# A hybrid encoder layer on one core: when the second half of the cross-attention keys is loaded and split, and where the normalisation of the memory is applied

## The chip, the cores and the metric

The kernel runs on one core of a Trainium2 chip. The metric is the device time of one execution in microseconds (us). In this text PE is TensorE, DVE is VectorE, ACT is ScalarE, POOL is GpSimd and SP is SyncE, the engine whose queue issues most of the loads. Each engine works through its own queue strictly in order; what waits at the head of a queue holds all that stands behind it.

## The reference

One layer with three residual sub-layers, on 1024 rows of width 1024 and a memory of 256 tokens, all in float32:

```python
mem_n = rms_norm(mem, mem_g)
y_ssm = s5_mixer(u, ...)                      # state space branch, 512 channels
y_fox = forgetting_attention(q, k, v, f_logit) # 8 heads of 64, causal
y_mix = concat([rms_norm(y_ssm), rms_norm(y_fox)])
x = x + rms_norm(y_mix @ w_out, mix_post_g)

h = rms_norm(x, xa_pre_g)                     # 4 heads of 256, 256 memory tokens
kv = mem_n @ wkv                              # keys: first 1024 columns, values: the rest
p = softmax((h @ wq) @ k.T / sqrt(256))
x = x + rms_norm((p @ v) @ wo, xa_post_g)

h = rms_norm(x, ffn_pre_g)
x = x + rms_norm((silu(h @ w_gate) * (h @ w_up)) @ w_down, ffn_post_g)
```

`rms_norm(mem)` multiplies each memory token by one number, the reciprocal root of its mean square, and each column by a gain. The number of a token is a constant of a whole column of `kv` transposed, so it can be applied to the memory before the product `mem_n @ wkv` or to the product behind it.

## The kernel before, in words

Every float32 product is made of three products of halves: a tile is *split* (`split`, L112 to L119) into a high part, rounded by ACT (L113), and a low part, the difference, made by DVE (L115, or L117 where a gain is multiplied in), and `mm3` (L121 to L124) adds high x high, high x low and low x high in one PSUM bank. So each tile that PE reads costs ACT and DVE one instruction each, and PE waits for the later of the two.

The program runs in stages: the input projection with the state space scan, the eight heads of the forgetting attention (their scores run from 231.8 to 468 us), the output projection (its additions run from 494.6 to 551.6 us), the cross attention, and the feed-forward part, which takes the rest. The attention heads are paced with *fillers*, other work that is stepped between them: among these `mem_load` (L955), which reads the memory, the sixteen `mem_tile`s (L971), each of which makes one 128-row tile of `kv` transposed and stores it in DRAM (`kv_d`), and `build_a(0)`.

`mem_load` first spreads the 256 reciprocal roots over all partitions (`row_bcast`, L169, two transposes on PE and an ACT copy, into a tile `rb` of the tag `t2`). Then for each of the eight slices of the memory DVE multiplies by `rb` in place (L965), and the slice is split with its gain (L113, L117). In `mem_tile` a weight tile is loaded and split (`load_w`, L155; its load is L159 and its tile `raw`, the split tile `whl`), 24 matmuls fill a bank, ACT copies it to a tile `t` (L977), and POOL issues the store.

The cross attention needs its query weights folded with the keys, `build_a(c)` for the two halves c of the heads (L1001), and its output weights folded with the values, `value_weights(h)` for the four heads (L1041). `build_a` loads the keys of a head from `kv_d` (L1008), splits them, loads and splits two tiles of query weights, and makes eight f32 tiles in four banks, each split with a gain into a `slab`. `build_a(0)` is one of the fillers. `value_weights(0)` and `(1)` are stepped between the halves of the output projection's tiles (L1054 to L1091); `value_weights(2)`, `build_a(1)` and `value_weights(3)` come at its end.

The loop over the output projection (L1060) goes through the tiles 3, 4, 5, 6, 7, 0, 1, 2. Each tile loads the state space part into `t` (tags `a` and `b` in turn, L1070) and the rows of `x` into `xt` (tags `e` or `c`, L1073), does two times twelve matmuls, adds (L1080), squares (ACT, L1082), multiplies by a gain (POOL, L1084), takes the reciprocal root (`rsqrt_mean`, ACT L137 and L138, DVE L139 to L145) and forms the residual (DVE, L1088). Tiles 3 to 7 are stored (POOL, L1092), tiles 0 to 2 stay in SBUF. Tile 7, the last one in the tag `e`, is stored from there.

The order of each engine's queue isn't written by hand: a scheduler sets it when the program is built, by its own estimates of time and by priorities, and the queues are then fixed. `tc.issue_after(i)` tells it that an instruction has to stand behind `i` in the order in which they are issued; it makes no wait at run time. Tiles come from pools with a fixed number of buffers for each tag: 2 of `a`, 2 of `b`, 3 of `c`, 1 of `d`, 1 of `e`, 3 of `t2`, 2 of `yt`, 2 of `raw`, 3 of `whl`, and 4 banks of `g`. An instruction that writes a tile waits for the last reader of the buffer's previous tile.

Of the kernel before, what the change touches and what calls it, by code (L numbers as in the profile page):

```python
# [10 lines left out]
F32R = mybir.dt.float32r  # L11
# [6 lines left out]
P = 128  # L18
S = 1024
D = 1024  # L20
# [32 lines left out]
def layer(ctx: ExitStack, tc: tile.TileContext, a, out):  # L53
# [113 lines left out]
        return v[:, 0], v[:, 1]  # L167

    def row_bcast(r, n):  # L169
        rb = t2t([P, n * P]) if n == 2 else tt("d", [P, n * P])  # L170
        ps = (s_ps if n > 4 else g_ps)([P, n * P])
        for j in range(n):
            pe.transpose(ps[:, j * P:(j + 1) * P], r[:, j:j + 1].broadcast_to([P, P]), ident)
        for j in range(0, n, 4):
            cs = slice(j * P, min(j + 4, n) * P)
            act.activation(out=rb[:, cs], in_=ps[:, cs], func=AF.Copy)
        return rb
# [778 lines left out]
    def mem_load(r, out):  # L956
        rb = row_bcast(r, 2)
        yield
        mh, ml = slab([P, KT, 256]), slab([P, KT, 256])
        for k in range(0, KT, 4):  # L960
            m = raw([P, 4, 256])
            sp.dma_start(out=m, in_=a["memT"].rearrange("(k p) m -> p k m", p=P)[:, k:k + 4])
            for kk in range(4):
                with behind():
                    dve.tensor_tensor(out=m[:, kk], in0=m[:, kk], in1=rb, op=ALU.mult)  # L965
                    split(mh[:, k + kk], ml[:, k + kk], m[:, kk], g_mem[:, k + kk:k + kk + 1])
                if kk % 2:
                    yield
        out.extend((mh, ml))

    def mem_tile(i, mh, ml):  # L971
        wh, wl = load_w(a["wkv"][i], P, stage="e" if i % 3 == 2 else None)
        ps = g_ps([P, 256])
        for k in range(KT):
            mm3(ps, wh[:, k], wl[:, k], mh[:, k], ml[:, k], k == 0, k == KT - 1)
        o = t2t([P, 256])
        act.activation(out=o, in_=ps, func=AF.Copy)  # L977
        stB.dma_start(out=kv_d[i], in_=o)


# [16 lines left out]
        yield from build_a(0)  # L997

    Ah, Al = {}, {}

    def build_a(c):  # L1001
        for t in range(2):
            Ah[c, t], Al[c, t] = slab([P, 4, 512]), slab([P, 4, 512])
        for h in range(2):
            hd = 2 * c + h
            kh = tt(("ea", "ba")[c][h], [P, 2, 2, 256], F32R)
            kr = kh[:, 1].bitcast(F32)
            sp.dma_start(out=kr, in_=kv_d[2 * hd:2 * hd + 2].rearrange("d p m -> p d m"))  # L1008
            split(kh[:, 0], kh[:, 1], kr)
            wq = [load_w(a["wqT"][2 * hd + d], P) for d in range(2)]  # L1010
            ms = slice(h * 256, h * 256 + 256)
            for ft in range(0, KT, 2):
                ps = g_ps([P, 2, 256])
                for f in range(2):
                    for d in range(2):
                        mm3(ps[:, f], wq[d][0][:, ft + f], wq[d][1][:, ft + f], kh[:, 0, d], kh[:, 1, d], d == 0, d == 1)
                for f in range(2):
                    split(Ah[c, ft // 4][:, ft % 4 + f, ms], Al[c, ft // 4][:, ft % 4 + f, ms], ps[:, f],
                          g_xa[:, ft + f:ft + f + 1])
                yield  # L1020
# [44 lines left out]
    for n, j in enumerate((3, 4, 5, 6, 7, 0, 1, 2)):  # L1065
        ts = slice(j * P, (j + 1) * P)
        t = tt("ab"[n % 2])
        with tc.issue_after(wo_read.ins) if n else ExitStack():
            for i in range(2):
                sp.dma_start(out=t[64 * i:64 * i + 64], in_=t1_d.rearrange("j (k s) d -> s k j d", s=16)[2 * j + i])  # L1070
        xt = tt("ec"[n % 4 > 0])
        with tc.issue_after(wo_read.ins):
            sp.dma_start(out=xt, in_=a["x"][ts, :])  # L1073
        ss4, ss, r = sm(4, "ss4"), sm(1, "ss"), sm(1, "r")
        for h in range(2):
            hs = slice(h * 512, h * 512 + 512)
            ps = x_ps([P, 512])
            for k in range(4):
                mm3(ps, yf[k][:, 0, ts], yf[k][:, 1, ts], wo[k][:, 0, hs], wo[k][:, 1, hs], k == 0, k == 3)
            dve.scalar_tensor_tensor(out=t[:, hs], in0=ps, scalar=r_f[:, j:j + 1], in1=t[:, hs], op0=ALU.mult, op1=ALU.add)  # L1080
            for q in range(2 * h, 2 * h + 2):
                act.activation(out=tt("yt", [P, 256]), in_=t[:, q * 256:q * 256 + 256], func=AF.Square,  # L1082
                               accum_out=ss4[:, q:q + 1])
            pool.tensor_tensor(out=t[:, hs], in0=t[:, hs], in1=g_mp[:, hs], op=ALU.mult)  # L1084
            step(between)
        dve.tensor_reduce(out=ss, in_=ss4, op=ALU.add, axis=mybir.AxisListType.X)
        rsqrt_mean(r, ss, D)
        dve.scalar_tensor_tensor(out=xt, in0=t, scalar=r, in1=xt, op0=ALU.mult, op1=ALU.add)  # L1088
        if j < 3:
            kept[j] = xt  # L1090
        else:  # L1091
            stC.dma_start(out=x1_d[j], in_=xt)  # L1092
# [546 lines left out]
```

## Time and profile before

| | |
|---|---|
| median of three runs | 1417.84 us (1416.02 to 1421.99) |
| the profiled execution, whole | 1418.36 us |
| its span in the profile | 1416.6 us |
| mean granted clock of PE | 0.989 of full speed |
| PE busy in the span | 97% |
| DVE, ACT, POOL busy | 67%, 46%, 27% |

PE is busy for nearly the whole span, and the stages differ in what the other engines have to do, so a share of the whole says little about one place. The rows of a timeline give the start, the duration, the engine, the line, the operation and the tiles (written<-read); a bracket at a row's end tells how long the engine had been idle before it and what released it. Rows with SPq are the moments at which SP's queue issues a transfer. Durations of matmuls are those of one from its first row to its last result and overlap; the distance of two starts is what one costs.

### The profile page before, as it was taken

To read this page: it belongs to the slowest core of one execution; us is meant where nothing else is said; L and a number is where in the kernel's file an instruction comes from. 1 tells how busy PE (TensorE), PEld (TensorE's weight loads), DVE (VectorE), ACT (ScalarE), POOL (GpSimd) and SP (SyncE) were. 2 spreads that over 40 slices of the span, in tenths; PEclk is the share of its full clock that TensorE was granted. 3 is DMA by queue.
4 is the path that set the end of the run, shared out by engine and by line. 5 is a ranking of instruction groups with operands and counts; after the bars stand their busy time and mean duration, and the time that the engine had idled before them with its cause. 6 is when DMAs were issued, how large, how long until landed. Compare 5 with 4: busy or idle time off the path is not lost.

```text
span 1416.6 us, 19877 instructions
## 1 busy us (share of the span) xinstructions
PE 1378.3 (97%) x7161; PEld 1150.5 (81%) x7161; DVE 949.1 (67%) x1719; ACT 650.1 (46%) x1273; POOL 377.3 (27%) x430
## 2 busy tenths in 40 slices
PE   9999989999999996999999999999999999999997
PEld 7889888779978785888888788888888888888886
DVE  8949944947667676535457677777766676565566
ACT  7383345856556545534334533333333334444441
POOL 0011110001111152002021367676666661000021
PEclk9999999989999998999999999999999999999999
DMA  6435665348672764024457255554444446965544
GB/s 216 150 109 154 208 221 136 96 130 237 192 198 87 220 207 138 31 74 149 164 175 270 97 186 186 182 189 147 151 156 156 169 151 223 336 225 196 179 164 164
DMA packets 104627, 241.52 MB, mean 170 GB/s; under 512 B 11528, under 2 KB 40200, under 8 KB 104336
## 3 DMA queue, kind: packets, MB, share of 16 engines
q1 hardware_dynamic: 86000, 178.33, 40.1%
q0 software_dynamic: 18528, 61.91, 12.1%
q8 instruction: 56, 0.92, 0.3%
q14 instruction: 43, 0.35, 0.1%
HBM read 171.52 MB, written 79.43 MB: 177 GB/s over the span
## 4 chain that ended last, share of the span: by engine, by line
PE 59%; ACT 0%; DVE 0%; DMA 0%; issue 0%; DVEq 0%; ACTq 0%
PE x L1304 17%; PE g L1304 13%; PE x L1567 7%; PE g L1567 7%; PE g L124 2%; PE g L122 2%; PE g L123 2%; PE x L122 2%; PE x L124 2%; PE x L123 2%; PE g L1100 1%; PE g L1211 1%; DMA raw<-in_wqT 0%; ACT whl L113 0%; DVE whl L115 0%
## 5 line engine op out<-in xcount | busy, mean ns | idle before, releaser
L1304 PE MATMUL x<-slab,op 128*128 128x512 f32 x984 | 233.2, 389 | 0.5 <-DVE op L115 0.5
L1304 PEld LDWEIGHTS x<-slab,op 128*128 128x128 f32 x984 | 184.6, 188 | 39.3 <-DVE op L115 1.0
L1304 PE MATMUL g<-slab,op 128*128 128x512 f32 x744 | 178.7, 389 | 0.0
L115 DVE TENSOR_TENSOR slab<-slab 128x1024 fp32r<-128x1024 f32 (+2 forms) x96 | 115.1, 1208 | 83.1 <-ACT slab L113 81.6
L1304 PEld LDWEIGHTS g<-slab,op 128*128 128x128 f32 x744 | 139.6, 188 | 29.0
L122 PE MATMUL g<-slab,whl 128*128 128x512 f32 (+1 forms) x416 | 151.6, 364 | 0.8 <-ACT slab L487 0.4
L123 PE MATMUL g<-slab,whl 128*128 128x512 f32 (+1 forms) x416 | 148.4, 357 | 0.0
L124 PE MATMUL g<-slab,whl 128*128 128x512 f32 (+1 forms) x416 | 148.3, 357 | 0.0
L113 ACT ACTIVATE slab<-slab 128x1024 fp32r<-128x1024 f32 (+2 forms) x96 | 99.3, 1039 | 103.7 <-DMA slab<-hs_d 78.1
L1567 PE MATMUL g<-slab 128*128 128x512 f32 x462 | 126.7, 389 | 0.0
L1567 PE MATMUL x<-slab 128*128 128x512 f32 x462 | 126.7, 389 | 0.0
L1567 PEld LDWEIGHTS x<-slab 128*128 128x128 f32 x462 | 86.7, 188 | 18.0
L1567 PEld LDWEIGHTS g<-slab 128*128 128x128 f32 x462 | 86.7, 188 | 18.0
L115 DVE TENSOR_TENSOR op<-slab,op 128x512 fp32r<-128x512 f32 x80 | 85.6, 1080 | 11.2 <-ACT op L113 10.9
L1380 POOL TENSOR_TENSOR wt<-wt 128x256 f32<-128x256 f32 x88 | 81.5, 927 | 26.2 <-DMA wt<-in_w_down 22.8
L122 PEld LDWEIGHTS g<-slab,whl 128*128 128x128 f32 x416 | 78.7, 189 | 12.0 <-ACT whl L113 0.6
L124 PEld LDWEIGHTS g<-slab,whl 128*128 128x128 f32 x416 | 78.4, 189 | 11.6 <-DVE whl L115 0.2
L123 PEld LDWEIGHTS g<-slab,whl 128*128 128x128 f32 x416 | 78.7, 189 | 10.6
L113 ACT ACTIVATE op<-slab 128x512 fp32r<-128x512 f32 x80 | 50.2, 629 | 80.6 <-PE x L1304 38.6
L113 ACT ACTIVATE op<-ss 128x512 fp32r<-128x512 f32 x60 | 37.7, 631 | 91.9 <-PE g L1304 55.7
L115 DVE TENSOR_TENSOR whl<-raw,whl 128x1024 fp32r<-128x1024 f32 (+2 forms) x58 | 64.5, 1118 | 20.9 <-ACT whl L113 20.6
L1407 POOL TENSOR_TENSOR ss<-slab 128x512 f32<-128x512 f32 x40 | 62.2, 1554 | 58.3 <-DMA slab<-in_w_up 25.9
(395 smaller groups left out, 2891.7 us busy)
## 6 DMA issues: line engine op xcount, KB each, us to landing
hs_d<-ev POOLq DMA_DIRECT2D x77, 256.0 KB, 2.6
slab<-hs_d SPq DMA_DIRECT2D x35, 512.0 KB, 4.0
wt<-in_w_down SPq DMA_DIRECT2D x44, 256.0 KB, 3.5
wt_d<-wt POOLq DMA_DIRECT2D x22, 512.0 KB, 4.8
slab<-in_w_gate SPq DMA_DIRECT2D x20, 512.0 KB
slab<-in_w_up SPq DMA_DIRECT2D x20, 512.0 KB, 5.1
slab<-wt_d SPq DMA_DIRECT2D x20, 512.0 KB, 8.2
wd_d<-in_w_down SPq DMA_DIRECT2D x33, 256.0 KB, 4.8
```

The lines of the kernel that those rows point to most:

```text
L113: first = act.activation(out=hi, in_=src, func=AF.Copy, scale=1.0 if mul is None else mul)
L115: (lo_eng or dve).tensor_tensor(out=lo, in0=src, in1=hi.bitcast(F32), op=ALU.subtract)
L122: pe.matmul(ps, lh, rh, start=first, stop=False)
L123: pe.matmul(ps, lh, rl, start=False, stop=False)
L124: pe.matmul(ps, ll, rh, start=False, stop=last)
L1100: pe.transpose(tp[:, k], src[:, (k0 + k) * P:(k0 + k + 1) * P], ident)
L1211: turned = pe.transpose(tp[:, k], h3[:, (4 * n + k) * P:(4 * n + k + 1) * P], ident)
L1304: pe.matmul(ps, x[:, k], y[:, k], start=first and k + n == 0, stop=k == 3 and n == 2, skip_group_check=not first)
L1380: pool.tensor_tensor(out=o, in0=x, in1=y, op=ALU.subtract)
L1407: made[0] = pool.tensor_tensor(out=o, in0=x, in1=y, op=fn)
L1567: pe.matmul(banks[n][j], xo[:, u, js], wo[:, v], start=ends[0] and k == 0, stop=ends[1] and k == 2, skip_group_check=onto is not None)
```

## The change

Three edits. First, the second half of the keys (`build_a(1)`) uses the tile tags `e` and `b` instead of `b` and `a`, and its two loads are issued behind the last load of `x` in the output projection (`x_read[0]`), its two splits behind the last reciprocal root there (`x_read[1]`, the ACT instruction of L137 or L138 that comes first). Second, DVE's eight products L965 go; the row constant `rb` is kept until the last `mem_tile`, and the eviction of each of the sixteen banks, an ACT copy before, is a DVE product with `rb` (L976 in the new numbering). Third, `rb` moves from the tag `t2` to the tag `yt`. Behind the places of the diff the line numbers move by one to two.

```diff
     def row_bcast(r, n):
-        rb = t2t([P, n * P]) if n == 2 else tt("d", [P, n * P])
+        rb = tt("yt", [P, n * P]) if n == 2 else tt("d", [P, n * P])
...
             for kk in range(4):
                 with behind():
-                    dve.tensor_tensor(out=m[:, kk], in0=m[:, kk], in1=rb, op=ALU.mult)
                     split(mh[:, k + kk], ml[:, k + kk], m[:, kk], g_mem[:, k + kk:k + kk + 1])
...
-        out.extend((mh, ml))
+        out.extend((mh, ml, rb))

-    def mem_tile(i, mh, ml):
+    def mem_tile(i, mh, ml, rb):
...
         o = t2t([P, 256])
-        act.activation(out=o, in_=ps, func=AF.Copy)
+        dve.tensor_tensor(out=o, in0=ps, in1=rb, op=ALU.mult)
         stB.dma_start(out=kv_d[i], in_=o)
...
+    x_read = [None, None]
...
-            kh = tt(("ea", "ba")[c][h], [P, 2, 2, 256], F32R)
+            kh = tt(("ea", "eb")[c][h], [P, 2, 2, 256], F32R)
             kr = kh[:, 1].bitcast(F32)
-            sp.dma_start(out=kr, in_=kv_d[2 * hd:2 * hd + 2].rearrange("d p m -> p d m"))
-            split(kh[:, 0], kh[:, 1], kr)
+            with tc.issue_after(x_read[0].ins) if c else ExitStack():
+                sp.dma_start(out=kr, in_=kv_d[2 * hd:2 * hd + 2].rearrange("d p m -> p d m"))
+            with tc.issue_after(x_read[1].ins) if c else ExitStack():
+                split(kh[:, 0], kh[:, 1], kr)
...
-            sp.dma_start(out=xt, in_=a["x"][ts, :])
+            x_read[0] = sp.dma_start(out=xt, in_=a["x"][ts, :])
...
-        rsqrt_mean(r, ss, D)
+        x_read[1] = rsqrt_mean(r, ss, D)[0]
```

What the scheduler makes of it shows in the queues. The first place is ACT's queue at the end of the output projection, before the change. The splits of keys write `a` and `b` (128x512); the split that writes `t_5682` belongs to the values of the third head (`value_weights(2)`); `yt,ss<-a` and `yt,ss<-b` are the squares of the last two tiles, `slab<-g` an eviction of `value_weights`.

```order
L113 ACTIVATE a<-a 128x512
L137 ACTIVATE rsy<-ss,epsc 128x1
L138 ACTIVATE rsy<-rsy 128x1
L1082 ACTIVATE yt,ss_5550<-a 128x256 x2
L113 ACTIVATE whl<-raw 128x1024
L1082 ACTIVATE yt,ss_5550<-a 128x256 x2
L113 ACTIVATE b<-b 128x512
L137 ACTIVATE rsy<-ss,epsc 128x1
L138 ACTIVATE rsy<-rsy 128x1
L113 ACTIVATE slab<-g 128x512
L1082 ACTIVATE yt,ss_5618<-b 128x256 x2
L113 ACTIVATE t_5682<-t_5683 128x512
```

The same place after the change. The values' split is now `t_5674`, the keys' tiles are `e` and `b`.

```order
L138 ACTIVATE rsy<-rsy 128x1
L113 ACTIVATE slab<-g 128x512
L1084 ACTIVATE yt,ss_5610<-b 128x256 x2
L113 ACTIVATE t_5674<-t_5675 128x512
L113 ACTIVATE whl<-raw 128x1024
L113 ACTIVATE slab<-g 128x512
L1084 ACTIVATE yt,ss_5610<-b 128x256 x2
L113 ACTIVATE slab<-g 128x512
L137 ACTIVATE rsy<-ss,epsc 128x1
L113 ACTIVATE slab<-g 128x512
L138 ACTIVATE rsy<-rsy 128x1
L113 ACTIVATE e<-e 128x512
```

The first split of keys stood eleven rows ahead of the values' split, the second five; now both stand behind it, eight and nine rows (the second, `b<-b`, follows the last row shown).

The second place is SP's queue there, before the change. `c<-in_x` are the last two loads of `x`, `a<-kv_d` and `b<-kv_d` the keys, `raw<-in_wqT` a tile of query weights, `t_5835` the values of the fourth head.

```order
L1073 DMA c<-in_x 128x1024
L1008 DMA a<-kv_d 128x2x256
L1073 DMA c<-in_x 128x1024
L1008 DMA b<-kv_d 128x2x256
L159 DMA raw<-in_wqT 128x1024
L1044 DMA t_5835<-kv_d 128x2x256
L159 DMA raw<-in_wo 128x1024
```

After the change:

```order
L1075 DMA c<-in_x 128x1024 x2
L1009 DMA e<-kv_d 128x2x256
L1009 DMA b<-kv_d 128x2x256
L159 DMA raw<-in_wqT 128x1024
L1046 DMA t_5827<-kv_d 128x2x256
L159 DMA raw<-in_wo 128x1024
```

One load of keys moved behind the last load of `x`, and the tiles are others; behind the keys the queue is the same.

The third place is DVE's queue where the memory is loaded, before the change. L965 is the product with the row constant, `slab<-raw,gains` the low half of a slice, `sv_s<-g` the copy of a sum of squares out of a bank, L743 the scaling of a softmax tile.

```order
L965 TENSOR_TENSOR raw<-raw,t_2765 128x256 x4
L742 RECIPROCAL nlr<-nlr 128x1
L117 SCALAR_TENSOR_TENSOR slab<-raw,gains,slab 128x256 x3
...
L117 SCALAR_TENSOR_TENSOR slab<-g,gains,slab 128x256
L742 RECIPROCAL nlr<-nlr 128x1
L117 SCALAR_TENSOR_TENSOR slab<-raw,gains,slab 128x256 x2
L743 TENSOR_SCALAR c<-c,nlr 128x896
L240 COPY sv_s<-g 128x8
```

After the change:

```order
L742 RECIPROCAL nlr<-nlr 128x1
L117 SCALAR_TENSOR_TENSOR slab<-raw,gains,slab 128x256 x2
...
L117 SCALAR_TENSOR_TENSOR slab<-g,gains,slab 128x256
L742 RECIPROCAL nlr<-nlr 128x1
L743 TENSOR_SCALAR c<-c,nlr 128x896
L117 SCALAR_TENSOR_TENSOR slab<-raw,gains,slab 128x256 x2
L115 TENSOR_TENSOR whl<-raw,whl 128x1024
L240 COPY sv_s<-g 128x8
```

The products are gone, and the low half of a weight tile (`whl`, L115) has come to stand directly ahead of the copy `sv_s`. In the memory tiles themselves each ACT row L977 is gone and a DVE row L976 stands in its place. From the middle of the cross attention on the queues are the same as before.

## The prediction

> **What bounds the kernel now.** I read the page first, then who TensorE (PE) waits for in the first 600 us, then stretches, then each queue's timeline around the longest wait.
>
> ```profile
> PE 1378.3 (97%) x7161; PEld 1150.5 (81%) x7161; DVE 949.1 (67%) x1719; ACT 650.1 (46%) x1273; POOL 377.3 (27%) x430
> ```
>
> PE is busy for 1378.3 of 1416.6 us. So only two things can be won: some 38 us in which it stands, and stretches in which its clock is halved. The waits of PE up to 600 us:
>
> ```profile
> PE g L122 <- ACT t L113: 10.8, 1, 10.8
> PE g L760 <- DVE sv_s L240: 1.8, 1, 1.8
> PE g L239 <- ACT slab L765: 1.8, 1, 1.8
> PE g L122 <- ACT slab L765: 1.4, 1, 1.4
> ```
>
> One wait of 10.8 us stands out (place B, the end of the output projection). The three others lie within 10 us of each other (place A, where the memory is loaded). The same in stretches; the last three columns are the granted clock, the DMA share and GB/s:
>
> ```profile
> 539.00:556.00 17.00, 6.18 (x17) 4.55 (x16) 12.34 (x21) 9.62 (x29) 7.81 (x4) 0.60 0.32 97
> 278.00:293.00 15.00, 10.10 (x44) 7.69 (x46) 10.23 (x25) 10.00 (x20) 1.08 (x2) 0.66 0.57 167
> 331.00:403.00 72.00, 72.00 (x583) 65.51 (x583) 45.88 (x91) 40.33 (x81) 11.64 (x19) 1.00 0.72 211
> 541.00:542.00 1.00, 0.00 (x0) 0.00 (x0) 0.94 (x2) 0.42 (x3) 0.00 (x0) 0.91 0.00 0
> 555.00:556.00 1.00, 1.00 (x4) 0.80 (x4) 0.00 (x0) 0.57 (x2) 0.00 (x0) 0.77 0.72 213
> ```
>
> At both places the clock falls as well (0.60, 0.66). In the memory tiles (331 to 403, place M) PE never stands. Now B, PE first:
>
> ```profile
> 538.90 0.39 PE L123 MATMUL g<-whl,t 128*128 128x512 f32 x1
> 539.13 0.39 PE L124 MATMUL g<-whl,t 128*128 128x512 f32 x1
> 550.34 0.80 PE L122 MATMUL g<-whl,t 128*128 128x512 f32 x1 [10.82 <-ACT t L113]
> 550.93 0.63 PE L123 MATMUL g<-whl,t 128*128 128x512 f32 x1
> 551.36 0.63 PE L122 MATMUL g<-whl,t 128*128 128x512 f32 x1
> 558.30 0.28 PE L122 MATMUL g<-b,whl 128*128 128x256 f32 x1
> 561.09 0.39 PE L124 MATMUL g<-b,whl 128*128 128x256 f32 x1 [0.84 <-DVE whl L115]
> 565.16 1.03 PE L1100 MATMUL g<-ident,c 128*128 128x128 f32 x8
> 572.30 0.39 PE L122 MATMUL g<-a,whl 128*128 128x256 f32 x1
> ```
>
> PE stops at 539.52 and resumes at 550.34, with 0.43 us from one matmul to the next where it had 0.23. The 0.91 of 541 to 542 means that the clock halves at about 541.8 (0.18 us at half makes 0.91). The 0.77 of 555 to 556 puts its return at about 555.5. What PE waits for is ScalarE's (ACT) split of the third head's values, and ACT had been held:
>
> ```profile
> 540.40 0.63 ACT L113 ACTIVATE a<-a 128x512 fp32r<-128x512 f32 x1 [10.02 <-DMA a<-kv_d]
> 549.67 0.61 ACT L113 ACTIVATE t<-t 128x512 fp32r<-128x512 f32 x1
> ```
>
> ACT stood 10.02 us (from 530.38) for a load of keys that PE first reads at 572.30 (`a,whl`), with the projection's evictions queued behind it. The loads come from SP:
>
> ```profile
> 528.14 0.38 SPq L1008 DMA_DIRECT2D a<-kv_d  x1
> 533.84 0.33 SPq L1073 DMA_DIRECT2D c<-in_x  x1
> 544.14 0.38 SPq L1008 DMA_DIRECT2D b<-kv_d  x1
> 546.35 0.33 SPq L159 DMA_DIRECT2D raw<-in_wqT  x1
> SPq L1008 <- DVE c L1088: 9.9, 1, 9.9
> ```
>
> The load took from 528.14 to 540.40, 12.3 us, behind others. SP then stood 9.9 us before the other half of the keys, whose buffer waited for the evictions that ACT held up.
>
> **The change part by part: B.** In the new order ACT's split `t<-t` has neither key split ahead of it. What else stands ahead of it is squares, two root pairs, a weight split and an eviction, some 6 us of ACT work between 530.4, where ACT fell idle (540.40 - 10.02), and 539.5, and PE's own matmuls feed it at the old pace. It must still wait for its buffer, whose last reader is the matmul of 539.13. So it starts at about 539.5, takes 0.61, and PE resumes at 540.2: 10.1 us are won. The remaining gap of 0.7 us is far below the 2.3 us after which the clock fell (539.52 to 541.8), so the half clock from 550.34 to 555.5 goes too: 5.1 us at half speed are 2.5 us. Gain so far 12.6.
>
> What is late next: the keys. Their two loads now stand behind both last loads of x, and the first needs tile `e`, which POOL is still storing:
>
> ```profile
> 529.21 0.60 POOL L1092 DMA_DIRECT2D x_d<-e  x1
> x_d<-e POOLq DMA_DIRECT2D x1, 512.0 KB, 7.7
> 542.83 1.28 DVE L1088 SCALAR_TENSOR_TENSOR c<-b,r,c 128x1024 f32<-128x1024 f32 x1
> 557.82 1.06 ACT L113 ACTIVATE whl<-raw 128x1024 fp32r<-128x1024 f32 x1
> 559.82 1.22 DVE L115 TENSOR_TENSOR whl<-raw,whl 128x1024 fp32r<-128x1024 f32 x1
> ```
>
> The store lands at 529.21 + 7.7 = 536.9, so SP issues both key loads by 537.5 and the next weights (`in_wqT`) by 538. Everything that was in flight had landed by 541, so I put the keys' landing at 542 to 543 and the weights' at 545. PE reaches the keys at 540.2 + 24 x 0.23 = 545.7. ACT has the key splits done by then (two of 0.63 behind the first evictions); the weight split ends at about 547.1 and VectorE's (DVE) low half at about 549.5, since the key subtractions (2 x 0.7) and a 1.3 us residual stand ahead of it. PE can do 6 of its 48 matmuls of 0.12 us (half of 0.23 for half the columns) with the first weight tile alone, to 546.4, and 9 more without the second's low half. That makes stalls of 0.7 (to 547.1) and 1.3 (548.2 to 549.5), or 2.0 where 0.84 stood: a loss of 1.2. Bounds: nothing, and the 6 us of the first rival below. The moved loads cost SP nothing else: behind them in its queue stand only those weights, the next head's values and its weights.
>
> **A.** Eight DVE products go:
>
> ```profile
> L965 DVE TENSOR_TENSOR raw<-raw,t x8: 410/419/422, 273.6 to 277.0; 128x256 f32<-128x256 f32 x8
> 281.38 0.33 SPq L159 DMA_DIRECT2D raw<-in_wkv  x1
> 283.64 0.16 DVE L240 COPY sv_s<-g 128x8 f32<-128x8 f32 x1
> 284.84 1.06 ACT L113 ACTIVATE whl<-raw 128x1024 fp32r<-128x1024 f32 x1 [0.71 <-DMA raw<-in_wkv]
> 286.53 0.80 PE L122 MATMUL g<-whl,slab 128*128 128x512 f32 x1 [1.35 <-ACT slab L765]
> 282.00:283.00 1.00, 0.06 (x1) 0.00 (x0) 1.00 (x4) 0.38 (x1) 0.00 (x0) 0.70 0.78 119
> ```
>
> That is 8 x 0.419 = 3.4 us out of a DVE queue that is full (1.00 of 282 to 283) and ends in the copy `sv_s`, which frees a PSUM bank for PE. But the order now puts a weight split (1.2 us, with its load and ACT's half before it) ahead of that copy. Its buffer comes free about 5 us earlier without the products; load 3.5 us (281.38 to 284.84), ACT 1.06, DVE 1.2 lead to a copy at about 282.9, 0.75 earlier. ACT's weight split then no longer stands between the copy and the eviction for which PE waits at 286.53: another 1.06. Gain 1.8. The clock had halved in 282 to 283 (0.70), some 4.5 us after PE's last long matmul; the thin stretch still lasts over 6 us, so I take nothing for the clock. Bounds: 0, and the whole jam (second rival).
>
> **M.** Sixteen ACT copies become DVE products, their row constant now held until the last tile:
>
> ```profile
> L977 ACT ACTIVATE t<-g x16: 360/364/369, 331.1 to 402.6; 128x256 f32<-128x256 f32 x16
> L115 DVE TENSOR_TENSOR slab<-g,slab 128x512 fp32r<-128x512 f32 x2 | 1.4, 688 | 0.7 <-ACT slab L113 0.7
> L115 DVE TENSOR_TENSOR t<-t,t 128x512 fp32r<-128x512 f32 x1 | 0.7, 685 | 0.0
> ```
>
> A product from PSUM costs DVE what one from SBUF does (688 against 685 ns), so I price it as the old one: 16 x 0.42 = 6.7 us. DVE goes from 45.88 to some 52.6 of 72 us beside a PE that is always busy; ACT loses 5.8. The softmax units run two ahead, which hides it. If that cover is gone, all 6.7 lie on the path; less than nothing isn't possible, as PE has no idle time there. Nearest row: PE 72.00 of 72.00. I take a loss of 0.5.
> [...]
>
> Sum: 12.6 - 1.2 + 1.8 - 0.5 = 12.7. The profiled execution took 1418.36 and would take 1405.7. The median of the three runs shown, 1417.84, is 0.5 lower, so I forecast 1405.2. (0.5%, 7.1 us, is about what a measurement of this kernel can tell from no change.)
>
> **The rivals.**
> *The wait moves to the keys.* If the first key load takes the 12.3 us of the old one, it lands at 549.2, PE waits from 545.7 to 549.8 and 1.9 more for the weights behind it, and the clock halves again (2.5). Of 12.6 then 4.1 stay; with A and M 5.4: 1412.5. For it: that transfer's row. Against: it was slow in a full queue, and the new one meets an empty one (DMA share 0.00 in 541 to 542). It decides from a landing after about 544.5. 0.13.
> [...]
> *The jam at A goes altogether*: waits 1.8 + 1.8 + 1.4 and about 3 us of half clock (286.53 to 292.7), 8 in place of 1.8: 1399. For it: DVE's queue was the limit. Against: the split now ahead of the copy. 0.12.
> *Not what it says*: issue order is no wait, and ACT may meet another late load before `t<-t`, so the long wait stays: 1416.5. Against: nothing ahead of it there waits for a load directly but one weight split, whose load was issued long before. 0.05.
> *Slower*: at M each product waits in DVE's in-order queue for the tile's last matmul, with the softmax of the next units behind it, and PE then waits for those. To end 0.5% slower it must cost (12.7 + 0.5 + 7.1) / 16 = 1.3 us of PE per tile; at 1.5 the time is 1428. For it: DVE was already 1.00 busy in parts. Against: 20 us of spare DVE time there, and ACT stood for none of the copies it replaces. 0.04.
>
> **How the numbers follow.** Forecast 0.66, with 1402 to 1409 as its own range (A 0 to 3, keys 0 to 3, M 0 to 2). The range of 8 in 10 goes on to the jam's case and the keys' case: 1399 to 1412.5. Faster: 0.66 + 0.12 = 0.78. Same: both cases near 1412 to 1416, 0.17. Slower 0.05.
>
> **What would show it.** Right: in the new trace ACT's `t<-t` starts within 1 us of the matmul that frees its buffer, the gap at B is about 0.7 with clock 1.00, the key splits run after the first evictions of the third head, and a PE wait of about 2 us stands before or in the keys' matmuls. At A the copy `sv_s` comes about 1 us sooner. Wrong: a wait of several us on `e<-kv_d` or `in_wqT` at the keys, a gap over 2.3 us at B, or PE waiting in the memory tiles for DVE.

## The result, and the profile after

The changed kernel takes 1405.64 us (median of 5 runs, 1402.18 to 1407.31), the kernel before beside it 1416.02 us (5 runs, 1414.55 to 1421.99): a ratio of 0.9915, with a 95% interval of 0.989 to 0.9941. The forecast was 1405.2. The span of the profiled execution went from 1416.6 to 1403.9 us, 12.7 less, which is the sum that was forecast; but the terms of that sum were not all right, and some of the 12.7 is chance: the two medians, taken side by side, differ by 10.4. (A correction to the section on the change: `x_read[1]` is the second ACT instruction of the reciprocal root, L138.)

PE's busy time on the page is what it was, so what went is idle time in the balance (B's matmuls take 1.5 us less, since the clock stays up there, and those of the heads up to the 14th mask take 1.6 us more, 38.09 for 36.50, with the clock at 0.96 there for 1.00); the second view is the waits of PE in the changed kernel (time in all, times, longest).

```profile
PE 1378.3 (98%) x7161; PEld 1150.4 (82%) x7161; DVE 956.5 (68%) x1727; ACT 645.0 (46%) x1257; POOL 379.1 (27%) x430
```

```profile
PE g L124 <- DVE t L115: 1.6, 2, 1.1
PE g L760 <- ACT d L784: 1.0, 1, 1.0
PE g L122 <- DVE slab L115: 0.6, 1, 0.6
PE g L122 <- ACT t L113: 0.6, 1, 0.6
PE g L122 <- ACT slab L765: 0.6, 1, 0.6
```

The wait for ACT's `t`, 10.8 us before, is 0.6. The waits of 1.8 for `sv_s` and 1.8 for L239 are gone, the 1.4 for `slab` L765 is 0.6, and a 1.0 for `d` L784 has come. To see what each place gave, both traces need marks that don't move. The heads' mask matmuls (L735) are 64 in both; these are the first, the 14th, the 21st and the last, before and then after, and the first transpose behind the keys (before: the row of 565.16 in the prediction).

```profile
231.98 0.23 PE L735 MATMUL s<-maskb,identb 128*128 128x128 bf16 x1
269.95 0.23 PE L735 MATMUL s<-maskb,identb 128*128 128x128 bf16 x1
306.83 0.23 PE L735 MATMUL s<-maskb,identb 128*128 128x128 bf16 x1
461.83 0.23 PE L735 MATMUL s<-maskb,identb 128*128 128x128 bf16 x1
```

```profile
230.92 0.23 PE L735 MATMUL s<-maskb,identb 128*128 128x128 bf16 x1
270.47 0.23 PE L735 MATMUL s<-maskb,identb 128*128 128x128 bf16 x1
304.15 0.23 PE L735 MATMUL s<-maskb,identb 128*128 128x128 bf16 x1
459.56 0.23 PE L735 MATMUL s<-maskb,identb 128*128 128x128 bf16 x1
552.52 0.71 PE L1102 MATMUL g<-ident,c 128*128 128x128 f32 x5
```

The distances between them, for all kernels of this study (us; the last column is the span less the last mark):

| kernel | to 1st mask | 1st to 14th | A: 14th to 21st | heads' rest: 21st to 64th | B: 64th to transposes | rest |
|---|---|---|---|---|---|---|
| before | 231.98 | 37.97 | 36.88 | 155.00 | 103.33 | 851.4 |
| after | 230.92 | 39.55 | 33.68 | 155.41 | 92.96 | 851.4 |
| keys_only | 229.00 | 37.97 | 36.62 | 156.07 | 92.72 | 851.1 |
| mem_only | 231.96 | 37.95 | 34.17 | 155.62 | 103.25 | 851.0 |
| tags_only | 229.29 | 37.97 | 34.05 | 156.83 | 101.76 | 851.2 |
| splits_only | 228.62 | 37.98 | 33.36 | 158.30 | 92.91 | 851.3 |
| clock_fill | 228.82 | 39.57 | 36.67 | 155.97 | 104.08 | 851.3 |
| clock_fill2 | 231.61 | 37.96 | 37.52 | 154.68 | 102.36 | 851.4 |
| mem_heavy | 231.93 | 37.97 | 34.08 | 155.28 | 96.00 | 851.1 |
| pool_scale | 229.51 | 39.54 | 37.45 | 155.90 | 102.16 | 851.1 |
| copy_first | 228.71 | 39.53 | 33.65 | 155.56 | 92.34 | 851.1 |
| query_behind | 229.48 | 38.01 | 33.05 | 155.30 | 103.65 | 851.6 |
| query_later | 229.10 | 37.97 | 33.79 | 154.03 | 93.32 | 851.2 |
| all_orders | 228.41 | 38.00 | 32.75 | 154.04 | 93.29 | 851.2 |

The first two columns hold no edit of the change, and they vary by 3.6 and 1.6 us on their own. So of the 12.7 us, B gave 10.4 and A 3.2, the heads' rest took 0.4, and chance took 0.5 (1.1 won before the heads, 1.6 lost at their start). The other columns vary without an edit, too: B is 102.16 to 103.33 in before, mem_only and pool_scale, which are alike there, and the heads' rest 154.68 to 155.97 in before, clock_fill and clock_fill2, which are alike in it. So the 0.4 can't be told from chance, and B's gain is known to about 1 us.

B in the changed kernel, in order of time: SP's load of the first keys, ACT's split of the third head's values and of the first keys, and all stops of PE in the stretch (the first of them belongs to the second head's values; before the change it is 0.59 us).

```profile
536.35 0.38 SPq L1009 DMA_DIRECT2D e<-kv_d  x1
```

```profile
537.76 0.62 ACT L113 ACTIVATE t<-t 128x512 fp32r<-128x512 f32 x1
543.34 0.62 ACT L113 ACTIVATE e<-e 128x512 fp32r<-128x512 f32 x1
```

```profile
516.86 0.74 PE L124 MATMUL g<-whl,t 128*128 128x512 f32 x2 [1.10 <-DVE t L115]
538.43 0.50 PE L122 MATMUL g<-whl,t 128*128 128x512 f32 x1 [0.62 <-ACT t L113]
540.61 0.72 PE L124 MATMUL g<-whl,t 128*128 128x512 f32 x2 [0.51 <-DVE t L115]
545.97 0.39 PE L122 MATMUL g<-e,whl 128*128 128x256 f32 x1 [0.26 <-ACT whl L113]
547.33 0.39 PE L122 MATMUL g<-e,whl 128*128 128x256 f32 x1 [0.62 <-DVE slab L115]
548.47 0.39 PE L124 MATMUL g<-e,whl 128*128 128x256 f32 x1 [0.28 <-DVE whl L115]
```

The split starts at 537.76, within 0.1 us of the moment at which PE stops (538.43 - 0.62 = 537.81), without a wait for a load, and PE stops for 0.62 us. The keys' stops are 0.26 + 0.62 + 0.28 = 1.16 where 0.84 stood. The stretch from the end of the heads to the transposes as a whole, before and after (PE busy first; third from last the granted clock):

```profile
482.33:565.16 82.83, 70.58 (x346) 58.03 (x346) 52.51 (x95) 36.77 (x118) 30.90 (x23) 0.92 0.63 184
```

```profile
480.07:552.52 72.45, 69.06 (x346) 56.27 (x345) 52.97 (x95) 36.21 (x118) 29.15 (x23) 1.00 0.70 211
```

The same 346 matmuls stand idle for 12.25 us before and 3.39 after, and are busy 1.52 us less, since the clock stays up. A as a whole, before and after:

```profile
269.95:306.83 36.88, 31.96 (x183) 24.11 (x181) 23.28 (x64) 23.95 (x54) 2.17 (x4) 0.86 0.47 143
```

```profile
270.47:304.15 33.68, 31.94 (x182) 24.02 (x181) 20.99 (x56) 23.60 (x54) 2.17 (x4) 0.90 0.52 157
```

PE is busy for the same time, so all of A's gain is time in which it stood. The stops after the change, PE and then DVE:

```profile
282.55 1.61 PE L760 MATMUL g<-ident,c 128*128 128x128 f32 x5 [1.00 <-ACT d L784]
284.74 0.79 PE L122 MATMUL g<-whl,slab 128*128 128x512 f32 x1 [0.58 <-ACT slab L765]
```

```profile
282.33 1.22 DVE L115 TENSOR_TENSOR whl<-raw,whl 128x1024 fp32r<-128x1024 f32 x1
283.47 0.16 DVE L240 COPY sv_s<-g 128x8 f32<-128x8 f32 x1
```

The weight tile's low half stands right ahead of the copy, as the order showed. In the memory tiles:

```profile
331.00:403.00 72.00, 70.83 (x568) 64.03 (x568) 51.77 (x108) 37.27 (x67) 11.75 (x19) 1.00 0.70 207
```

```profile
L976 DVE TENSOR_TENSOR t<-g,yt 128x256 f32<-128x256 f32 x16 | 6.8, 423 | 7.5 <-PE g L124 7.2
```

DVE is busy for 51.77 of 72 us (45.88 before, 52.6 forecast). PE stands 1.17 us here, all of it in one stop for the softmax at 402.45, behind the tiles; before, that stop is 0.95 us at 404.70, outside of the window.

### The profile page after: what moved, and what is told of

It is laid out like the page before. It is cut to its first block, busy times and chain, and to the rows that moved or that the text cites. A ratio compares the mean times of both kernels' runs of the same rounds, so it can differ in the third digit from the quotient of the medians.

```text
span 1403.9 us, 19877 instructions
## 1 busy us (share of the span) xinstructions
PE 1378.3 (98%) x7161; PEld 1150.4 (82%) x7161; DVE 956.5 (68%) x1727; ACT 645.0 (46%) x1257; POOL 379.1 (27%) x430
## 3 DMA queue, kind: packets, MB, share of 16 engines
q0 software_dynamic: 18528, 61.91, 12.3%
## 4 chain that ended last, share of the span: by engine, by line
PE 60%; DVE 1%; ACT 0%; DMA 0%; issue 0%; DVEq 0%; ACTq 0%
PE x L1306 17%; PE g L1306 13%; PE x L1569 7%; PE g L1569 7%; PE g L124 2%; PE g L122 2%; PE g L123 2%; PE x L122 2%; PE x L123 2%; PE x L124 2%; PE g L1102 1%; PE g L1213 1%; DMA raw<-in_wqT 0%; DVE whl L115 0%; ACT whl L113 0%
## 5 line engine op out<-in xcount | busy, mean ns | idle before, releaser
L115 DVE TENSOR_TENSOR slab<-slab 128x1024 fp32r<-128x1024 f32 (+2 forms) x96 | 115.3, 1208 | 82.3 <-ACT slab L113 80.1
L115 DVE TENSOR_TENSOR op<-slab,op 128x512 fp32r<-128x512 f32 x80 | 88.5, 1117 | 10.4 <-ACT op L113 10.1
L123 PEld LDWEIGHTS g<-slab,whl 128*128 128x128 f32 x416 | 79.0, 190 | 10.7
L115 DVE TENSOR_TENSOR whl<-raw,whl 128x1024 fp32r<-128x1024 f32 (+2 forms) x58 | 66.0, 1144 | 18.4 <-ACT whl L113 18.1
```

What stands on the lines that cost most here:

```text
L115: (lo_eng or dve).tensor_tensor(out=lo, in0=src, in1=hi.bitcast(F32), op=ALU.subtract)
L123: pe.matmul(ps, lh, rl, start=False, stop=False)
```

## The experiments

The theory: ACT works in order, a split that waits for a load holds all behind it (10.02 us in the kernel before), and B's gain comes from the place of the key splits alone. The rivals: the tiles and SP's order do it; the keys become late; DVE is held in the memory tiles.

**keys_only**: the changed kernel with the three memory edits undone (products L965 back, eviction by ACT, `rb` in `t2`).

> The edits of the keys alone; the memory is scaled as before the change. Theory (ACT's in-order queue: a split that waits for a load holds the values' split behind it): the whole gain at the end of the output projection, 10.4 us by the trace of the changed kernel, and none at the memory: a ratio to the kernel before of about 0.9925, PE's gap before the third head's values under 1 us, the waits of 1.8, 1.8 and 1.4 at the memory load back. Rival (the gain needs both parts, because the memory tiles now end earlier): under 8 us, and a wait of more than 2 us at the keys.

Measured: 1406.9 us, ratio 0.9941 (0.9919 to 0.9962). B takes 92.72, 10.6 less than before; A 36.62, as before. PE's gap before the third head's values is 1.56 us, not under 1, and the waits at the memory load are 1.8, 1.0 and 2.1. For B's gain the theory holds, and the parts don't need each other.

**mem_only**: the changed kernel with the key edits undone (tags `ba`, no `issue_after`).

> The edits of the memory alone; the keys are loaded and split as before the change. Theory: at the memory load 3.2 us are won and in the memory tiles 0.4 lost, 2.8 us in all or a ratio of 0.998, and the wait for the third head's values is back at 10 to 11 us. Rival: that wait shortens by more than 2 us too, because all loads come earlier.

Measured: 1414.81, ratio 0.9984 (0.9972 to 0.9996). A gains 2.7, the heads' rest loses 0.6, B is 103.25 with its wait of 10.9. As the theory has it.

**tags_only**: which edit of the keys it is.

```diff
-            with tc.issue_after(x_read[0].ins) if c else ExitStack():
-                sp.dma_start(out=kr, ...)
-            with tc.issue_after(x_read[1].ins) if c else ExitStack():
-                split(kh[:, 0], kh[:, 1], kr)
+            sp.dma_start(out=kr, ...)
+            split(kh[:, 0], kh[:, 1], kr)
```

> The changed kernel without the two orders behind x: the keys have the new tiles, their loads stand in SP's queue where the change puts them, but both splits stand ahead of the values' split in ACT's queue. Theory: ACT stands again, from about 529 until the loads of 536.4 have landed (about 541), PE's gap is 8 to 11 us, and the time is within 3 us of the kernel before less the 2.8 of the memory part: 1413 to 1418. Rival (what counts is that SP and the tile buffers are no longer held): a gap under 3 us and about 1407.

Measured: 1411.23, ratio 0.996 (0.9946 to 0.9975), a little under the theory's range of times, and a gap a little under its 8 us. The load by SP, the split by ACT and PE's stop:

```profile
536.33 0.38 SPq L1008 DMA_DIRECT2D e<-kv_d  x1
```

```profile
539.25 0.63 ACT L113 ACTIVATE e<-e 128x512 fp32r<-128x512 f32 x1 [5.71 <-DMA e<-kv_d]
```

```profile
545.10 0.80 PE L122 MATMUL g<-whl,t 128*128 128x512 f32 x1 [7.17 <-ACT t L113]
```

SP's order is that of the changed kernel, and PE still stops for 7.17 us: B gains only 1.6. The load landed 2.9 us after its issue, not 12.3: the first rival of the prediction falls with that.

**splits_only**: the reverse; of the key edits only the place of the splits is kept.

```diff
-            kh = tt(("ea", "eb")[c][h], [P, 2, 2, 256], F32R)
+            kh = tt(("ea", "ba")[c][h], [P, 2, 2, 256], F32R)
...
-            with tc.issue_after(x_read[0].ins) if c else ExitStack():
-                sp.dma_start(out=kr, ...)
+            sp.dma_start(out=kr, ...)
```

> The changed kernel with the old tiles for the keys (b and a) and their loads not ordered behind x: of the key edits only the splits' place in ACT's queue is left. Theory: the splits' place is all, so the time is that of the changed kernel, 1404 to 1407, with stalls of at most 2 us at the keys. Rival (tiles and loads matter too): SP stands for the buffer of b again, the weights behind it come late, and PE waits 3 us or more at the keys: 1409 or more.

Measured: 1403.84, ratio 0.9912 (0.9891 to 0.9933), just under the theory's 1404. The second load of keys and the values' split:

```profile
532.55 0.39 SPq L1008 DMA_DIRECT2D b<-kv_d  x1
```

```profile
536.42 0.62 ACT L113 ACTIVATE t<-t 128x512 fp32r<-128x512 f32 x1
```

B takes 92.91. SP no longer stands long for the buffer of `b`, because ACT no longer holds the evictions that free it: this load is issued 0.42 us after the load of `x` ahead of it (532.13), where SP stood 9.9 us before the change. New tiles and the loads' order bring nothing: the place of the two splits is the whole of B. (The edit moves the DVE half of each split with the ACT half; that ACT's half is what counts is read from the rows, where ACT waits for the load and PE for ACT.)

**clock_fill** and **clock_fill2**: the price of the half clock. The kernel before, with matmuls that fill PE's gap.

```diff
         for c in range(2):
             tiles = [...]
+            if h == 2 and c == 0:
+                for _ in range(40):                      # 52 in clock_fill2
+                    pe.matmul(tiles[0][1], yf[0][:, 0, 0:P], wo[0][:, 0, 0:512], start=True, stop=True)
             for d in range(2):
```

> The kernel before, with 40 more matmuls that PE does while it waits for the third head's values (their bank is overwritten by the product that follows; nothing is left out). The wait for ACT stays as long, but PE doesn't idle through it. Theory (the half clock behind the gap costs 2.5 us): the granted clock stays at 1.00 from 541 to 556, the values' product takes about 5.5 us in place of 8.0 up to the keys, the keys wait no more than 1 us longer, and the ratio is 0.998 to 0.999. Rival (the keys behind it wait for the other engines anyway): the stall before the keys' low half grows from 0.8 to over 2.5 us, and nothing is won.

Measured: 1417.33, ratio 0.9991 (0.9978 to 1.0004). It did not test what it should: PE still stopped twice, and the clock fell at about 550.

```profile
549.32 0.50 PE L122 MATMUL g<-whl,t 128*128 128x512 f32 x1 [2.16 <-ACT t L113]
551.71 0.80 PE L124 MATMUL g<-whl,t 128*128 128x512 f32 x1 [1.66 <-DVE t L115]
```

```profile
550.00:552.00 2.00, 0.34 (x2) 0.29 (x2) 2.00 (x3) 1.61 (x6) 1.39 (x2) 0.52 0.00 0
```

> As clock_fill, with 52 such matmuls in place of 40: 11.8 us of them from 537.9 to about 549.7, so that PE has no idle stretch over 2 us at the end of the output projection (40 left 2.2 and 1.7 us close together, and the clock fell all the same). Theory (the half clock there cost 1.5 to 2.5 us in the kernel before): the granted clock stays at 1.00 to the keys, and the stretch from the end of the heads to the transposes of the cross attention takes 81 to 82 us where it took 82.8 before. Rival (what is behind it waits for the other engines anyway): 82.5 us or more at full clock.

Measured: 1418.08, ratio 0.9997 (0.998 to 1.0013). Now the clock stays at 1.00:

```profile
541.00:556.00 15.00, 13.87 (x61) 11.18 (x60) 12.95 (x24) 9.77 (x31) 7.93 (x4) 1.00 0.31 84
```

The stretch from the end of the heads takes 81.85 (82.83 before): B gains 1.0, the upper part of the theory's range. That is one profile of each, and no more than B varies without an edit. A closer measure is from ACT's split of the third head's values to the transposes: 15.49 us in before, with 5.1 us of PE's work at half clock; 14.72 and 14.70 in mem_only and pool_scale, which are alike there but have 3.5 us of it; 14.25 here, with none. So with the engines' order as before the half clock cost some 0.5 to 1.2 us, not 2.5: a PE at full clock waits for the low half of the values instead (1.13 us here).

**mem_heavy**: the point from which DVE decides in the memory tiles.

```diff
-        dve.tensor_tensor(out=o, in0=ps, in1=rb, op=ALU.mult)
+        for _ in range(3):
+            dve.tensor_tensor(out=o, in0=ps, in1=rb, op=ALU.mult)
```

> The changed kernel, with each of the sixteen evictions of the memory tiles done three times over: 32 more DVE products of 0.42 us, 13.4 us. Theory (DVE has some 20 us to spare in that stretch and the softmax runs ahead): DVE is busy for about 65 of 72 us there and PE loses under 2 us. Rival (each product holds DVE's in-order queue up to the tile's last matmul, with the softmax behind it): 8 to 14 us are lost, 1413 to 1419.

Measured: 1404.6, ratio 0.9899 (0.9877 to 0.9922).

```profile
L977 DVE TENSOR_TENSOR t<-g,yt 128x256 f32<-128x256 f32 x48 | 20.1, 419 | 6.1 <-PE g L124 5.5
```

```profile
331.00:403.00 72.00, 71.24 (x572) 64.02 (x569) 60.09 (x137) 37.58 (x69) 11.57 (x19) 1.00 0.70 207
```

Thirty-two more products cost the heads' rest nothing (155.28 against 155.41), with DVE busy for 60.09 us where 65 was expected. The rival falls. But B took 96.0 in this profile, 3.0 more than in the changed kernel, with no edit there: PE stops for 0.60, 1.39 and 0.52 us, and the clock falls at 541.9. At 0.66 over 5 us the fall is worth up to 1.7 of the 3.0.

```profile
541.00:546.00 5.00, 4.48 (x14) 3.32 (x13) 3.37 (x7) 2.19 (x8) 1.80 (x1) 0.66 0.65 202
```

The profiled run, 1408.27, is the slowest of the four.

**pool_scale**: is it DVE's time that counts in A? The kernel before, with L965 on POOL.

```diff
-                    dve.tensor_tensor(out=m[:, kk], in0=m[:, kk], in1=rb, op=ALU.mult)
+                    pool.tensor_tensor(out=m[:, kk], in0=m[:, kk], in1=rb, op=ALU.mult)
```

> The kernel before, with the eight products with the row constant done by POOL, which is idle there, instead of DVE; nothing else of the change. Theory (what cost at the memory load was DVE's full queue): the stretch of the memory load takes 33.5 to 35 us, as in the changed kernel, where it took 36.9. Rival (what cost was the product standing in the chain from the load to the split): 36 us or more.

Measured: 1419.87, ratio 1.0004 (0.9987 to 1.002); A takes 37.45. The rows of POOL, of DVE and of ACT:

```profile
271.74 7.41 POOL L965 TENSOR_TENSOR raw<-raw,t 128x256 f32<-128x256 f32 x8 [40.85 <-ACT t L176]
```

```profile
274.60 0.95 DVE L117 SCALAR_TENSOR_TENSOR slab<-raw,gains,slab 128x256 fp32r<-128x256 f32 x1
```

```profile
284.99 1.06 ACT L113 ACTIVATE whl<-raw 128x1024 fp32r<-128x1024 f32 x1 [3.44 <-DMA raw<-in_wkv]
```

The theory's forecast failed, but the run doesn't isolate the cause: beside POOL, two of the eight low halves on DVE take 0.95 us where they took 0.48, and ACT stands 3.44 us for a weight load ahead of the evictions that PE waits for. What is shown is that without the products A gains 2.7 to 3.8 us (seven kernels without another edit there, with A between 33.05 and 34.17); which of DVE's time, the chain to the split and ACT's order gives how much of it stays open.

**copy_first**: what is left in A. The first memory tile's weights are split behind the reciprocal root of the state space rows.

```diff
     def glu_stats():
-        rsqrt_mean(r_s, sv, 512, 4 * EPS)
+        rs_done.append(rsqrt_mean(r_s, sv, 512, 4 * EPS)[0])
...
-        wh, wl = load_w(a["wkv"][i], P, stage=...)
+        wh, wl = load_w(a["wkv"][i], P, stage=..., after=None if i else rs_done[0])
```

> The changed kernel, with the split of the first memory tile's weights ordered behind the reciprocal root of the state space branch, so that it no longer stands ahead of the copy of the sums. Theory (what is left of the wait at the memory load is that split in ACT's and DVE's queues): PE's waits of 1.0 and 0.6 there fall to 0.5 or less in all and the half clock gets shorter, 1 to 3 us won against the changed kernel, unless they are given back at about 400 us. Rival (PE waits for the softmax there in any order): no more than 0.3 us won.

Measured: 1402.87, ratio 0.9887 (0.987 to 0.9904), but A takes 33.65, as in the changed kernel. The rival is right for A:

```profile
280.32 1.27 PE L762 MATMUL g<-ident,c 128*128 128x128 f32 x5 [1.00 <-DVE sv_s L240]
```

The wait for `d` has gone, and one of the same 1.00 us for the copy has come in its place: two waits had ended together, and the slices of the memory still stand ahead of the copy on DVE. The lower time isn't A's: in its profile 2.2 of the 3.0 us against the changed kernel lie ahead of the heads, where nothing was edited.

**query_behind** and **query_later**: the heads' rest took longer in most kernels that came earlier to it, also in keys_only, which has no memory edit. The stop for the softmax near 400 us is in the kernel before, too (0.95 us), and without an edit there it is 0.63 in clock_fill2 and 1.95 in clock_fill. In splits_only, where it lost most (158.30), ACT and PE show why:

```profile
396.27 1.06 ACT L113 ACTIVATE whl<-raw 128x1024 fp32r<-128x1024 f32 x1 [5.66 <-DMA raw<-in_wqT]
```

```profile
399.31 0.51 PE L732 MATMUL s<-slab,a 128*128 128x512 f32 x1 [2.21 <-DVE nlr L739]
```

It is the mechanism of B once more: the split of the query weights for the first keys stands in ACT's queue ahead of the softmax. The edit to the changed kernel:

```diff
-            wq = [load_w(a["wqT"][2 * hd + d], P) for d in range(2)]
+            wq = [load_w(a["wqT"][2 * hd + d], P, after=None if c else last[-1]) for d in range(2)]
                        # query_later: after=None if c or h else last[-15]
```

> The changed kernel, with the splits of the query weights of the first half of the keys ordered behind the last softmax exponential, as far as it is emitted there. In every trace so far ACT stands 4 to 6 us at about 395 us for the load of such a weight tile, which PE reads much later, and PE then waits 1.0 to 2.6 us for the softmax. Theory (the same mechanism as with the keys): that wait of PE falls under 0.4 us and 1 to 2 us are won against the changed kernel. Rival (the late splits make PE wait at the keys' products): a wait of over 1 us for whl between 405 and 470 us, and nothing won.

Measured: 1412.78, ratio 0.9963 (0.995 to 0.9975). The wait at 400 us has gone, but B's column loses 10.7, at the end of the heads:

```profile
458.03 0.39 PE L124 MATMUL g<-a,whl 128*128 128x256 f32 x1 [1.58 <-DVE whl L115]
466.72 3.26 PE L774 MATMUL g<-slab 128*64 128x256 f32 x16 [3.12 <-ACT slab L765]
```

The splits moved by more than forty rows; the wait moved with them, and the clock fell there (0.67 over 460 to 470 us). The rival came true.

> The changed kernel, with the split of the first tile of query weights moved by three rows only, behind the exponentials of the third and the fourth tile of that head's softmax (query_behind moved it by 46 rows, past the due time of its raw buffer, and lost 10 us there). Theory: PE's wait of 1.2 to 2.6 us at about 400 us falls under 0.4, and the memory tiles' stretch, 99.1 us in the changed kernel, becomes 97.5 to 98.3: a time of 1402 to 1404. Rival (the softmax there waits for something else as well): no change, 1405 to 1406.

Measured: 1402.23, ratio 0.9895 (0.9873 to 0.9917). The stretch of 97.5 to 98.3 that was expected can't be read, since the mask matmul that ends it has moved; but the heads' rest takes 154.03 in place of 155.41, and PE doesn't wait between 380 and 410 us. A shift of three rows won 1.4 us against the changed kernel's profile; this kernel and the next have the shortest heads' rest of all fourteen, 0.6 us under the shortest of the others (154.68 in clock_fill2). The time of 1402 to 1404 came true, but not by this alone: the first two columns are 3.4 us lower as well.

**all_orders**: query_later, with two more orders.

```diff
-                with behind():
+                with tc.issue_after(evicted[1].ins) if k + kk in (4, 5) else behind():
                     split(mh[:, k + kk], ml[:, k + kk], ...)
...
-        wh, wl = load_w(a["wkv"][i], P, stage=...)
+        wh, wl = load_w(a["wkv"][i], P, stage=..., after=None if i else evicted[1])
```

> query_later, with two more orders at the memory load: the fifth and sixth slice of the memory and the first memory tile's weights are split behind the second eviction of the state space rows, so that neither stands ahead of the copy of the sums (copy_first moved only the weights, and PE then waited 1.0 us for the copy behind the slices). Theory (PE's waits there follow the order on ACT and DVE): waits of 0.6 us or less in all, the stretch of the memory load 32.5 us or less where the changed kernel takes 33.7, query_later's gain kept, 1400 to 1402. Rival (the softmax moved behind the slices and the weights holds PE instead): a stretch of 33.5 or more, or a new wait of over 0.5 us at the scores.

Measured: 1399.81 us (6 runs, 1399.05 to 1406.53), ratio 0.9888 (0.9866 to 0.991), the fastest median of all.

```profile
277.75 1.33 PE L762 MATMUL g<-ident,c 128*128 128x128 f32 x5 [0.26 <-DVE sv_s L240]
279.56 0.79 PE L122 MATMUL g<-whl,slab 128*128 128x512 f32 x1 [0.47 <-ACT slab L767]
```

Waits of 0.7 in place of 1.6, and A takes 32.75, short of the 32.5 that was expected. From the 14th mask on it is 2.1 us faster than the changed kernel (1397.7 - 266.41 against 1403.9 - 270.47). The two intervals overlap (to 0.991, from 0.989), so the timed runs alone don't prove it.

## Why the prediction was right

**B, the held split: right.** ACT's `t<-t` met no load, PE's gap became 0.62 us (forecast 0.7), and 10.2 us went (10.1). splits_only shows that the place of the splits does it alone, tags_only that without it nearly nothing comes.

**B, the clock: right in kind, too large.** The clock stays at 1.00, but that is worth 1.5 us in the change (70.58 - 69.06) and some 0.5 to 1.2 alone (clock_fill2), not 2.5. The step took half of 5.1 us as won, as if nothing else could bind PE there. That the clock stays up was partly luck: the step took 2.3 us as the stop that it takes to fall, and in mem_heavy it fell at this place with no stop over 1.39 us. It stayed up there in the changed kernel, keys_only and splits_only (1.00 over the stretch in each). The last section has what the traces show of a fall.

**B, what is late next: too large, and one term missed.** The keys cost 1.16 - 0.84 = 0.3 us, not 1.2: they landed in 2.9 us (tags_only), and both halves of the first keys' split were done at 544.81, over 1 us before PE came to them at 545.97. Missed was the low half of the values on DVE, for which PE waits 1.6 us in all where it waited 0.6. Half of this 1.0 is the change's: the stop of 0.51 at the third head's values, 0.42 to 0.52 in all eight kernels with the new place of the splits, and absent before. The other half is chance: the stop at the second head's values is 1.10 for 0.59, and it is anything from none (clock_fill) to 1.22 (pool_scale) in kernels that are alike there. So B is 10.2 + 1.5 - 0.3 - 1.0 = 10.4 where 11.4 was forecast.

**A: too small.** 3.2 us for 1.8. The two terms of the forecast came out at about their size: PE's wait at L760 fell from 1.79 to 1.00 (0.75 forecast; it now ends with `d`, not with the copy), the one behind it from 1.35 to 0.58 (1.06 forecast). The copy came 0.7 us nearer to the 14th mask (13.00 for 13.69), as forecast, with some luck: the terms given for it (281.38 - 5 + 3.5 + 1.06 + 1.2) add up to 282.1 and not to 282.9. The step went wrong in leaving the wait of 1.8 for L239 where it was. It went. The half clock ended sooner, too, at 289.0 for 292.6, but PE's busy time in A is the same, so nothing of the gain is seen to come from that. The full jam (8 us) did not dissolve: two waits and the half clock stay.

**M: the mechanism is right, its 0.5 isn't shown.** The cover of the softmax holds, as the step said: PE stands nowhere in the memory tiles, and mem_heavy has three products for each one and loses nothing. The 0.4 us by which the heads' rest is longer lie within what it varies without an edit (154.68 to 155.97). What stop there is comes at the query weights' load near 400 us, before the change, too; no step of the prediction had seen it, and query_later takes it away. The product from PSUM takes 423 ns, 4 more than the old one from SBUF (419), so the price of 0.42 us for each was right.

The errors nearly cancelled: 10.4 + 3.2 - 0.4 = 13.2, less 0.5 of chance, is 12.7. That the total fits to 0.1 us is luck; what the runs bear out is B's mechanism and its size. (The chances of the cases add up to 0.18 for the same and 0.04 for slower, not to 0.17 and 0.05.) Of the rivals, the late keys fall with the 2.9 us of tags_only's load, and the slower one with mem_heavy.

## What to carry to other kernels

A load that came late cost most here where its consumer stood in an in-order queue ahead of work that others needed (ACT stood 10.02 us for the keys, and PE 10.82 us for the values' split behind them): look for waits on a DMA on the engine that evicts, and move that one consumer behind the urgent work, by a few rows and not by many (three rows won 1.4 us in query_later, more than forty lost 10.7 in query_behind); tiles and load order can stay (B takes 92.91 us in splits_only, 92.96 in the changed kernel). Before a wait is booked as gain, ask which wait ended at the same time behind it, on the other engine of the pair. And compare marks inside the traces, not only times: here two early stages moved by 3.6 and 1.6 us from profile to profile without any edit. A single profile of each kernel doesn't settle a difference of 1 us in a stage either: B moved by 1.2 us and the heads' rest by 1.3 on their own.

## What the runs showed of the hardware

The clock doesn't fall after one fixed length of a stop. In the traces of before and after its changes, down and up, stand whole multiples of 3.41 us apart, as on a grid whose place differs from one execution to the other. In before it changes at 190.2, 193.7, 282.4, 292.6, 541.8, 555.5 and 1412.2 us: these are 1, 26, 3, 73, 4 and 251 steps. In after it does at 190.1, 193.5, 234.4, 237.8, 282.2, 289.0 and 1401.8 us: 1, 12, 1, 13, 2 and 326 steps. The half clock in other traces fits this: 6.8 us in clock_fill (from 550.1) and in all_orders (from 277.8), 10.2 us in pool_scale (from 280.9), which are 2, 2 and 3 steps. The long stop of B took 2.3 us until the fall in before, 3.1 in pool_scale, 4.1 in mem_only and 4.7 in tags_only, where PE stops at 537.93 and this row puts the fall at 542.6:

```profile
542.00:543.00 1.00, 0.00 (x0) 0.00 (x0) 1.00 (x3) 0.44 (x3) 0.62 (x1) 0.81 0.00 0
```

The grid fits the start of the heads as well. With the same two stops of 0.57 and 0.90 us, the clock stayed up in the kernel before and fell in the changed one:

```profile
234.00:237.00 3.00, 2.10 (x13) 1.56 (x12) 2.71 (x10) 1.34 (x5) 0.00 (x0) 1.00 1.01 299
```

```profile
234.00:237.00 3.00, 2.74 (x9) 2.36 (x10) 2.01 (x9) 1.13 (x4) 0.00 (x0) 0.57 0.98 344
```

Four of the fourteen profiles have the fall at the heads (39.5 in the second column of the table where the others have 38.0), 1.6 us each time. In these four, one step of the grid holds both stops whole, in after that from 231.01 to 234.42 (the stops are 231.51 to 232.08 and 233.36 to 234.26). In before an edge at 234.61 lies inside the second stop, 234.42 to 235.32, and in six others an edge lies in the second stop or between the two (mem_only, tags_only, clock_fill2, mem_heavy, query_later, all_orders). In query_behind one step holds both by about 0.02 us, and the clock stayed up; in keys_only and splits_only the place of the grid isn't known. The step ahead of a fall needn't be idle from end to end: the one before the fall at 541.8 holds 1.1 us of matmuls, and the one at the heads in the changed kernel 1.9 us. How idle a step has to be isn't settled here.

While POOL multiplied (pool_scale), some of DVE's instructions took longer: 0.95 us for 0.48 in two low halves of the memory, 0.90 for 0.61 in a scaling of the softmax (L743, 128x768) and 1.21 for 0.75 in another low half (`slab<-t`, 128x512). Two of L739, which read the scores `s` that PE writes, took 0.95 and 1.08 us as before.
